# Where two buffers begin: padding ahead of y and of the sums of x in an encoder kernel

## The chip, the cores and the metric

The kernel runs on one core of a Trainium2 chip. The metric is the device time of one execution in microseconds; the median of three runs stands for a kernel. One further execution was taken with the hardware profiler, and the rows below come from it.

## The reference

The reference is the trunk of an encoder with two layers on x of 256 tokens by 1024 channels, all in float32. Each layer adds three terms to x:

```
x = x + 0.5 * swiglu(rmsnorm(x), w_gate, w_up, w_down)     # 1024 -> 2816 -> 1024
x = x + mixer(rmsnorm(x))
x = x + 0.5 * swiglu(rmsnorm(x), w_gate, w_up, w_down)
# swiglu(h) = (silu(h @ w_gate) * (h @ w_up)) @ w_down
```

The mixer of the first layer has one input projection to 2560 columns, a gated part with a 128 by 128 spatial matrix, dilated attention with 8 heads, and an output projection. The mixer of the second layer takes centred averages over windows of 2, 4, 8 and 16 tokens minus the token itself, maps each of four groups of channels by a matrix, and scales. The four networks (swiglu) are most of the work.

## The kernel before, in words

**Numbers.** TensorE runs on float32r operands. To keep float32 accuracy each operand is split into a high part and the rest (ScalarE copies the high part, VectorE subtracts it), and each product is three matmuls: high by high, high by rest, rest by high. `mm3` (line 756) has the weights stationary and 256 tokens moving; `mm3x` (line 763) has 128 tokens stationary and 512 columns of weights moving.

**Weights.** 147 chunks of 1 MB come from memory through SyncE's queue into six buffers `raw`; they are split into four pairs `wh`, `wl` of 8192 bytes per partition. x is kept split in `xh`, `xl`.

**The networks.** `ffn` (line 771 ff.) goes through the 22 blocks of 128 hidden columns by a plan of letters. H takes two blocks in the plain way: x stationary, gate and up columns of the weights moving, 512 at a time. S (`seven`, line 899) takes four blocks with seven products in place of eight, as Strassen and Winograd do: four of the seven products have **sums of x** (`combine`, line 712) as their stationary operand. These sums, four pairs of high part and rest, lie in a buffer named `combos`. There are 15 S blocks; each has 4 products x 4 blocks of rows x 3 matmuls with sums. The results become **y**, the hidden activations, transposed by TensorE (`turned`, line 809) and split into a buffer named `yb`. `down` (line 840) multiplies y by w_down with `mm3`: y moves, the weights are stationary.

**Other users of the two buffers.** In the even mixer (line 1011 ff.) `combos` holds queries, keys, values and gates, and `yb` the input of the output projection, which again moves against stationary weights. In the odd mixer (line 1246 ff.) `yb` holds the tokens' projections and `combos` the pooling matrix.

**Order.** A planner (class `Order`) emits the program. It estimates the time of every instruction from its count of elements, keeps a clock for each engine and puts each engine's instructions in the order in which their inputs are due. It knows nothing of addresses.

**Layout.** Buffers come from pools. Pools lie behind one another in each partition in the order in which they are opened; every buffer is rounded up to 32 bytes. A pool with bufs=n has n copies of each name, used in turn. The pools and their buffers, in bytes per partition:

| pool, in order | buffers |
|---|---|
| cst | raw 6 x 8192, wh and wl 4 x 2 x 8192, xh, xl, xg 8192 each, vec 240, X 8192, ident 512, mixer_consts 8192, acc 2048, ones 4, mhalf 64 |
| tmp, each twice | sq 2048, v 8, rs_y 64, rs_a 64, rs_r 64, half 16, ss 64, ssv 64, one 4 |
| tiny | st 24, four times |
| t2k_pool | t2k 2048, eight times |
| shared | yb 16384, combos 16384 |

`v` takes the mean square in a norm (line 667), `ssv` the same in the mixer, `one` is written once and never read (line 1210).

Of the kernel before, what the change touches and what calls it, by code (L numbers as in the profile page):

```python
# [9 lines left out]
F32 = mybir.dt.float32  # L10
F32R = mybir.dt.float32r
# [4 lines left out]
P = 128  # L16
D = 1024
S = 256
FF = 2816
KD = D // P  # L20
KF = FF // P
NT = S // P
# [16 lines left out]
EXTRA_AT = 2 * 33 + 33 + 14 + 1  # L39
PLANS = ("HHHHSSSH", "HHSSSSH", "HHSSSSH", "HHSSSSH")  # L40
ADD_ISSUE, ADD_TIME, ADD_LAG = 1.4, 5.9, 6.0


V_NORM = 0
# [43 lines left out]
class Order:  # L88
# [13 lines left out]
    def task(self, eng, fn, *deps, can=None, urgent=0.0, idle=0.0):  # L102
        t = Task(eng, fn, deps, can, urgent, idle)
        self.late[eng].append(t)
        return t
# [57 lines left out]
    def need(self, task, what=""):  # L163
        if task is not None:
            self.wait(lambda: task.end is not None and task.end <= self.t, what)
# [217 lines left out]
def tile_encoder(ctx: ExitStack, tc: tile.TileContext, x, w, vecs, qk_gain, w_sp, b_sp, rope, mask, pool_op, eye, out):  # L383
    nc = tc.nc

    cst = ctx.enter_context(tc.tile_pool(name="cst", bufs=1))
    tmp = ctx.enter_context(tc.tile_pool(name="tmp", bufs=2))
    tiny = ctx.enter_context(tc.tile_pool(name="tiny", bufs=4))
    t2k_pool = ctx.enter_context(tc.tile_pool(name="t2k_pool", bufs=8))
# [4 lines left out]
    xh = cst.tile([P, KD, S], F32R, name="xh")  # L394
    xl = cst.tile([P, KD, S], F32R, name="xl")
    xg = cst.tile([P, KD, S], F32, name="xg")
    shared = ctx.enter_context(tc.tile_pool(name="shared", bufs=1))
    ctx.enter_context(tc.manual_schedule())

    O = Order(nc)  # L400
# [8 lines left out]

    def t2k(a, b):  # L410
        return t2k_pool.tile([P, a, b], F32, name="t2k")

    def bank():
        return psum_a.tile([P, 512], F32, name="bank")

    def bank2():
        return psum_b.tile([P, 512], F32, name="bank2")
# [166 lines left out]
    ps = bank2()  # L584
    for _ in range(WARM):
        nc.tensor.matmul(ps[:, :S], lhsT=warm[:, :P], rhs=warm, start=True, stop=True)
    mhalf = cst.tile([P, 16], F32, name="mhalf")
    nc.gpsimd.memset(mhalf, -0.5)

    def mixer_loads():  # L590
# [20 lines left out]
    class Norm:  # L611
# [37 lines left out]
        def square(self, i, *deps, urgent=0.0, idle=0.0):  # L649
            sq = []  # L650

            def square():
                sq.append(self.acc if i == 0 else t2k(2, S))
                A.activation(sq[0], X[:, 2 * i:2 * i + 2], AF.Square)

            t = task("A", square, *deps, urgent=urgent, idle=idle)
            if i:
                t = task("V", lambda: V.tensor_add(self.acc, self.acc, sq[0]), t, urgent=urgent, idle=idle)
            self.summed.append(t)
# [4 lines left out]
                    E.matmul(ps[:, t:t + 1], lhsT=self.acc[:, j, t * P:(t + 1) * P], rhs=ones, start=j == 0, stop=j == 1)  # L664

        def mean(self, ps):
            self.v = tmp.tile([P, NT], F32, name="v")
            V.tensor_scalar(self.v, ps[:, :NT], 1.0 / D, EPS, op0=OP.mult, op1=OP.add)

        def columns(self):  # L670
# [41 lines left out]
        def combine(self, idle):  # L712

            a11, a12 = xg[:, :4, :P], xg[:, 4:, :P]
            a21, a22 = xg[:, :4, P:], xg[:, 4:, P:]
            made, used = [], []
            combos = self.sums_of_x = shared.tile([P, 8, 4, P], F32R, name="combos")

            def add(make, *deps):
                i = len(made)  # L720
                s = []

                def fn():
                    s.append(t2k(4, P))
                    make(s[0])
                    used.append(s)
                    if len(used) == 4:
                        W.raw.lend(XG, xg_raw, O.clock["V"])

                v = task("V", fn, *deps, *self.gained, idle=idle)  # L730
                h = task("A", lambda: A.activation(combos[:, 2 * i], s[0], AF.Copy), v, idle=idle)
                l = task("V", lambda: V.tensor_sub(combos[:, 2 * i + 1], s[0], f32(combos[:, 2 * i])), h, idle=idle)
                made.append(l)
                return s, v

            s1, v1 = add(lambda s: V.tensor_sub(s, a22, a21))
            s2, v2 = add(lambda s: V.scalar_tensor_tensor(s, s1[0], -1.0, a11, op0=OP.mult, op1=OP.subtract), v1)
            add(lambda s: V.tensor_sub(s, a11, a21))
            add(lambda s: V.scalar_tensor_tensor(s, s2[0], -1.0, a12, op0=OP.mult, op1=OP.subtract), v2)
            self.combos = made  # L740
# [22 lines left out]
    def mm3x(ps, xh, xl, wh, wl, first, last, more=False):  # L763

        E.matmul(ps, lhsT=xh, rhs=wh, start=first, stop=False, skip_group_check=more)
        E.matmul(ps, lhsT=xh, rhs=wl, start=False, stop=False, skip_group_check=more)
        E.matmul(ps, lhsT=xl, rhs=wh, start=False, stop=last, skip_group_check=more)
        O.run()


    def ffn(n, f, plan, nxt, store=False, soon=(), after_last_sums=None, squares_first=False):
# [5 lines left out]
            return ring.get()  # L777

        n.columns_soon(ring)
        yb = shared.tile([P, 2, 2, 4, S], F32R, name="yb")  # L780
        tok = [slice(t * P, (t + 1) * P) for t in range(NT)]

        def rows(u, k):
# [205 lines left out]
        for i in range(5):  # L989
            if i < 4:  # L990
                d = 2 * i
# [19 lines left out]
    def even_mixer(n, units, nxt):  # L1011
        B = Blocks(W, units)
        arena = shared.tile([P, 4096], F32, name="combos")
        cat = shared.tile([P, 2, KD, S], F32R, name="yb")
        ch, cl = cat[:, 0], cat[:, 1]
        used = [0]

# [11 lines left out]
        def at(step, *tasks):  # L1029
            B.at(step, *tasks)  # L1030
# [87 lines left out]
        def spatial(g, step):  # L1118
            a = {}

            def mix():
                ps = bank2()
                for t in range(NT):
                    E.matmul(ps[:, t * P:(t + 1) * P], lhsT=gv[t][:, g * P:(g + 1) * P], rhs=wsp[:, g, :],
                                     start=True, stop=True)
                m = t2k(NT, P)
                V.scalar_tensor_tensor(m, ps[:, :S].rearrange("p (t s) -> p t s", t=NT),
                                               vec[:, V_SGU + g:V_SGU + g + 1],
                                               bsp[:, g, None, :].to_broadcast([P, NT, P]), op0=OP.mult, op1=OP.add)
                a[0] = t2k(1, S)[:, 0]  # L1130
                V.tensor_mul(a[0], u[:, g], m.rearrange("p t s -> p (t s)"))
                A.activation(ch[:, g], a[0], AF.Copy)

            at(step, mix)
            at(step + 1, lambda: V.tensor_sub(cl[:, g], a[0], f32(ch[:, g])))
# [71 lines left out]
            at(26 + 2 * g, gate)  # L1207
        for g in range(GROUPS):
            spatial(g, 33 + 2 * g)
        one = tmp.tile([P, 1], F32, name="one")  # L1210
        at(36, lambda: A.activation(one, ones, AF.Exp))
        psv = []
        for t in range(NT):
# [14 lines left out]
        for i in range(KD // 2):  # L1228
# [10 lines left out]
            t = task("V", add, urgent=1.2)  # L1239
# [5 lines left out]

    def odd_mixer(n, units, nxt):
        B = Blocks(W, units)
        hw = shared.tile([P, NT, D], F32, name="yb")
        banks = []
        for g in range(4):  # L1250
            ps = bank()
            if g == 3:
                n.columns()
            need(n.ok[2 * g + 1], "x")
            wh, wl = B.take(4)
            for t in range(NT):
                for k in range(2):
                    kk, s, c = 2 * g + k, slice(t * P, (t + 1) * P), slice(k * 256, (k + 1) * 256)
                    mm3x(ps[:, t * 256:(t + 1) * 256], n.h[:, kk, s], n.l[:, kk, s], wh[:, c], wl[:, c], k == 0, k == 1)
            banks.append(ps)  # L1260
        B.close()
        for g in range(4):
            c = slice(g * 256, (g + 1) * 256)
            A.activation(hw[:, 0, c], banks[g][:, :256], AF.Copy, scale=n.col[:, 0:1])
            V.tensor_scalar(hw[:, 1, c], banks[g][:, 256:], n.col[:, 1:2], None, op0=OP.mult)
        m = Norm(nxt)
        op = extra[0].rearrange("p (t g s) -> p t g s", t=NT, g=4)
        first = P - max(WINDOWS) // 2
        for i in range(KD // 2):
            ps = bank2()  # L1270
            for e in (2 * i, 2 * i + 1):
                c, o = slice(e * P, (e + 1) * P), e % 2 * S
                E.matmul(ps[:, o:o + S], lhsT=hw[:, 0, c], rhs=op[:, 0, e // 2, :], start=o == 0, stop=False)
                E.matmul(ps[:, o + first:o + S], lhsT=hw[:, 1, c], rhs=op[:, 1, e // 2, first:], start=False,
                         stop=o > 0)
                O.run()

            def add(e, ps=ps):
                o = e % 2 * S
                V.scalar_tensor_tensor(X[:, e], ps[:, o:o + S], vec[:, V_POOL + e:V_POOL + e + 1], X[:, e],  # L1280
                                       op0=OP.mult, op1=OP.add)

            ts = [task("V", lambda e=e, add=add: add(e), urgent=0.6) for e in (2 * i, 2 * i + 1)]
            m.pair(i, *ts, urgent=0.6)
            m.square(i, *ts)
        return m
# [121 lines left out]
```

## Time and profile before

| | us |
|---|---|
| median of three runs | 844.29 |
| lowest and highest | 843.77, 845.03 |
| the profiled execution | 845.57 |
| its span, first to last instruction | 843.8 |
| TensorE busy in it | 831.0 |
| VectorE, ScalarE busy | 694.2, 530.5 |

A page of the profile gives busy times by engine, a row of 40 slices, DMA queues, the chain of work that ended last and the costliest groups of instructions. In the rows, PE is TensorE, PEld its loads of stationary operands, DVE is VectorE, ACT ScalarE, POOL GpSimd and SP SyncE. Nearly every instruction has line 196, a helper that records all operations, so rows are told apart by the names of their tiles: `bank<-wh,combos` is a matmul into a bank of the accumulator with wh moving and combos stationary (the moving operand is named first). The end of a matmul is modelled; its start is not.

### The profile page before, as it was taken

Reading aid. Unit: us, or ns where it says so; the run is one execution under the profiler, and the core shown is the slowest. Engines: PE = TensorE matmul, PEld = TensorE weight load, DVE = VectorE, ACT = ScalarE, POOL = GpSimd, SP = SyncE. Lnnn points to the kernel's source line nnn. Section 1 sums busy time; section 2 is a strip of 40 time slices with the busy share of each in tenths; the row PEclk is TensorE's granted clock in tenths of the full one; section 3 lists DMA queues with packets and bytes.
Section 4 is the critical chain, followed back from the end, with each engine's and each line's share of the span. In section 5 each row is a group of like instructions: output and inputs, shape, how many; then the busy total and the mean of one; then the engine's idle time right before and its main releaser. Section 6 shows DMA issues by size and latency. Waiting matters only on the chain.

```text
span 843.8 us, 12378 instructions
## 1 busy us (share of the span) xinstructions
PE 831.0 (98%) x4980; PEld 730.1 (87%) x4980; DVE 694.2 (82%) x655; ACT 530.5 (63%) x544; POOL 67.3 (8%) x53
## 2 busy tenths in 40 slices
PE   7999999999999999999999999999999999999998
PEld 6888888998887988898899888888889788889888
DVE  5956998968877689999986789998967899998972
ACT  7836676556648586756754676766755576765740
POOL 0110000002400011000000100010000100001000
PEclk9999999999999999999999999999999999999999
DMA  9999997965443788999988798999896398999901
GB/s 311 376 334 230 259 288 211 336 250 191 158 150 101 201 243 239 270 305 266 321 285 241 219 239 227 296 293 305 239 371 180 133 248 246 287 318 288 274 3 50
DMA packets 110714, 206.37 MB, mean 245 GB/s; under 512 B 5440, under 2 KB 26816, under 8 KB 108608
## 3 DMA queue, kind: packets, MB, share of 16 engines
q1 hardware_dynamic: 93728, 173.59, 60.1%
q0 software_dynamic: 15840, 31.46, 20.9%
q8 instruction: 39, 0.64, 0.3%
q10 hardware_dynamic: 1088, 0.52, 0.2%
q14 instruction: 19, 0.16, 0.1%
HBM read 204.50 MB, written 1.05 MB: 244 GB/s over the span
## 4 chain that ended last, share of the span: by engine, by line
PE 93%; DVE 3%; ACT 2%; issue 1%; DMA 1%; POOL 0%; SPq 0%; ACTq 0%; POOLq 0%
PE bank L196 93%; DVE wl L196 1%; DVE t2k L196 1%; ACT wh L196 1%; ACT t2k L196 1%; DMA raw<-w_in 1%; DMA X<-x_in 0%; DVE xl L196 0%; ACT L196 0%; DVE yb L196 0%; ACT xh L196 0%; DVE acc L196 0%; POOL rs_y L196 0%; DVE X L196 0%; ACT acc L196 0%
## 5 line engine op out<-in xcount | busy, mean ns | idle before, releaser
L196 DVE TENSOR_TENSOR wl<-raw,wh 128x2048 fp32r<-128x2048 f32 (+2 forms) x159 | 354.7, 2247 | 41.2 <-ACT wh L196 41.1
L196 ACT ACTIVATE wh<-raw 128x2048 fp32r<-128x2048 f32 (+2 forms) x159 | 297.5, 1880 | 108.9 <-PE bank L196 75.0
L196 PE MATMUL bank<-yb,wh 128*128 128x256 f32 x1536 | 275.0, 281 | 0.0
L196 PEld LDWEIGHTS bank<-yb,wh 128*128 128x128 f32 x1536 | 236.7, 188 | 5.0 <-issue 1.0
L196 PE MATMUL bank<-yb,wl 128*128 128x256 f32 x768 | 214.4, 279 | 0.0
L196 PE MATMUL bank<-wh,xh 128*128 128x512 f32 (+1 forms) x484 | 189.4, 391 | 0.9 <-ACT wh L196 0.7
L196 PE MATMUL bank<-wl,xh 128*128 128x512 f32 (+1 forms) x484 | 187.2, 387 | 1.7 <-DVE wl L196 1.7
L196 PE MATMUL bank<-wh,xl 128*128 128x512 f32 (+1 forms) x484 | 187.3, 387 | 0.0
L196 PE MATMUL bank<-wh,combos 128*128 128x512 f32 x480 | 160.9, 398 | 0.0
L196 PEld LDWEIGHTS bank<-yb,wl 128*128 128x128 f32 x768 | 144.3, 188 | 0.0
L196 PEld LDWEIGHTS bank<-wl,xh 128*128 128x128 f32 x484 | 91.0, 188 | 19.7 <-DVE wl L196 2.8
L196 PEld LDWEIGHTS bank<-wh,combos 128*128 128x128 f32 x480 | 90.2, 188 | 19.9
L196 PEld LDWEIGHTS bank<-wh,xl 128*128 128x128 f32 x484 | 90.9, 188 | 18.9
L196 PEld LDWEIGHTS bank<-wh,xh 128*128 128x128 f32 x484 | 91.0, 188 | 18.8 <-ACT wh L196 1.7
L196 PE MATMUL bank<-wl,combos 128*128 128x512 f32 x240 | 95.4, 397 | 0.0
L196 POOL DMA_DIRECT2D raw<-w_in x23 | 29.6, 1288 | 390.5 <-DMA raw<-w_in 134.2
L196 ACT ACTIVATE wh<-mixer_consts 128x2048 fp32r<-128x2048 f32 x22 | 42.1, 1914 | 26.9 <-PE bank L196 19.8
L196 DVE TENSOR_TENSOR wl<-mixer_consts,wh 128x2048 fp32r<-128x2048 f32 x22 | 50.3, 2286 | 10.1 <-ACT wh L196 10.1
L196 PEld LDWEIGHTS bank<-wl,combos 128*128 128x128 f32 x240 | 45.1, 188 | 11.4 <-DVE wl L196 2.1
L196 ACT ACTIVATE t2k<-bank 128x512 f32<-128x512 f32 x53 | 31.4, 593 | 32.0 <-PE bank L196 31.4
L196 ACT ACTIVATE t2k<-bank,rs_r 128x256 f32<-128x256 f32 (+1 forms) x51 | 28.0, 569 | 36.8 <-PE bank L196 36.4
L196 ACT ACTIVATE yb<-bank 128x512 fp32r<-128x512 f32 (+1 forms) x48 | 27.8, 579 | 26.0 <-PE bank L196 26.0
(94 smaller groups left out, 638.7 us busy)
## 6 DMA issues: line engine op xcount, KB each, us to landing
raw<-w_in SPq DMA_DIRECT2D x69, 1024.0 KB, 7.6
raw<-w_in SPq DMA_DIRECT2D x71, 512.0 KB, 8.1
raw<-w_in POOLq DMA_DIRECT2D x23, 1024.0 KB, 13.0
mixer_consts<-w_in SPq DMA_DIRECT2D x13, 1024.0 KB, 7.6
raw<-w_in SPq DMA_DIRECT2D x38, 256.0 KB, 6.2
raw<-w_in SPq DMA_DIRECT2D x23, 384.0 KB, 6.1
xg<-w_in SPq DMA_DIRECT2D x8, 1024.0 KB, 9.8
raw<-w_in SPq DMA_DIRECT2D x8, 768.0 KB, 7.5
```

The costliest lines, as they stand in the source:

```text
L196: return f(*args, **kw)
```

## The change

The pool `shared` is opened straight behind `cst`, ahead of `tmp`. `mhalf`, the last buffer of `cst`, becomes 96 bytes longer, and the buffer of y 64 bytes longer at its end; neither extra part is used. y's buffer gets one size for all its users, and each takes a view of it. To make room, `v` and `one` lose their own buffers and take those of `ssv`.

```diff
+AHEAD_Y, AHEAD_COMBOS = 96, 64
...
     cst = ctx.enter_context(tc.tile_pool(name="cst", bufs=1))
+    shared = ctx.enter_context(tc.tile_pool(name="shared", bufs=1))
     tmp = ctx.enter_context(tc.tile_pool(name="tmp", bufs=2))
...
-    shared = ctx.enter_context(tc.tile_pool(name="shared", bufs=1))
...
+    def y_buffer(dtype):
+        return shared.tile([P, 16 * S + AHEAD_COMBOS // 4], dtype, name="yb")[:, :16 * S]
...
-    mhalf = cst.tile([P, 16], F32, name="mhalf")
+    mhalf = cst.tile([P, 16 + AHEAD_Y // 4], F32, name="mhalf")
...
-            self.v = tmp.tile([P, NT], F32, name="v")
+            self.v = tmp.tile([P, NT], F32, name="ssv")
...
-        yb = shared.tile([P, 2, 2, 4, S], F32R, name="yb")
+        yb = y_buffer(F32R).rearrange("p (b h k s) -> p b h k s", b=2, h=2, k=4)
...
-        cat = shared.tile([P, 2, KD, S], F32R, name="yb")
+        cat = y_buffer(F32R).rearrange("p (h k s) -> p h k s", h=2, k=KD)
...
-        one = tmp.tile([P, 1], F32, name="one")
+        one = tmp.tile([P, NT], F32, name="ssv")[:, :1]
...
-        hw = shared.tile([P, NT, D], F32, name="yb")
+        hw = y_buffer(F32)[:, :NT * D].rearrange("p (t d) -> p t d", t=NT)
```

## Rows read from the trace of the kernel before

**Rows 1.** The page, busy time by engine; clock of TensorE and DMA in 40 slices
```profile
PE 831.0 (98%) x4980; PEld 730.1 (87%) x4980; DVE 694.2 (82%) x655; ACT 530.5 (63%) x544; POOL 67.3 (8%) x53
PEclk9999999999999999999999999999999999999999
DMA  9999997965443788999988798999896398999901
```

**Rows 2.** The page, the chain that ended last, share by engine
```profile
PE 93%; DVE 3%; ACT 2%; issue 1%; DMA 1%; POOL 0%; SPq 0%; ACTq 0%; POOLq 0%
```

**Rows 3.** The waits of TensorE (waiting instruction <- releaser: us, times, longest)
```profile
PE bank L586 <- ACT sq L583: 2.5, 1, 2.5
PE bank L196 <- DVE t2k L196: 2.4, 3, 1.1
PE bank L196 <- DVE wl L196: 1.7, 3, 0.8
PE bank L196 <- ACT yb L196: 1.3, 1, 1.3
PE bank L196 <- ACT wh L196: 0.7, 1, 0.7
```

**Rows 4.** Timeline of TensorE: start us, us, instruction; x stationary, 512 columns
```profile
63.96 0.39 PE L196 MATMUL bank<-wh,xh 128*128 128x512 f32 x1
...
67.59 0.39 PE L196 MATMUL bank<-wl,xh 128*128 128x512 f32 x1
```

**Rows 5.** Timeline of TensorE, x and weights with 256 columns
```profile
648.06 0.28 PE L196 MATMUL bank<-wl,xh 128*128 128x256 f32 x1
...
651.77 0.28 PE L196 MATMUL bank<-wh,xl 128*128 128x256 f32 x1
```

**Rows 6.** Timeline of TensorE, sums of x stationary, 512 columns
```profile
506.40 0.39 PE L196 MATMUL bank<-wh,combos 128*128 128x512 f32 x1
...
512.00 0.28 PE L196 MATMUL bank<-yb,wh 128*128 128x256 f32 x1
```

**Rows 7.** Timeline of TensorE, y moving; a trio is two rows
```profile
832.77 0.40 PE L196 MATMUL bank<-yb,wh 128*128 128x256 f32 x2
833.00 0.28 PE L196 MATMUL bank<-yb,wl 128*128 128x256 f32 x1
...
839.42 0.40 PE L196 MATMUL bank<-yb,wh 128*128 128x256 f32 x2
```

**Rows 8.** Groups of TensorE: tiles, shape, count | busy us, mean ns | idle
```profile
L196 PE MATMUL bank<-yb,wh 128*128 128x256 f32 x1536 | 275.0, 281 | 0.0
L196 PE MATMUL bank<-yb,wl 128*128 128x256 f32 x768 | 214.4, 279 | 0.0
L196 PE MATMUL bank<-wh,combos 128*128 128x512 f32 x480 | 160.9, 398 | 0.0
L196 PE MATMUL bank<-wl,combos 128*128 128x512 f32 x240 | 95.4, 397 | 0.0
L196 PE MATMUL bank<-ident,t2k 128*128 128x128 f32 x224 | 33.9, 274 | 2.4 <-DVE t2k L196 2.4
```

**Rows 9.** Timeline of TensorE, four transposes behind one another; one takes 0.274 (rows 8)
```profile
52.83 0.60 PE L196 MATMUL bank<-ident,t2k 128*128 128x128 f32 x4
```

**Rows 10.** Tiles rs_y, one, mhalf: xcount: ns min/median/max, first and last start us
```profile
L196 POOL TENSOR_TENSOR rs_y<-ssv,mhalf x3: 1635/3276/3345, 210.4 to 234.0; 128x16 f32<-128x16 f32 x2, 128x8 f32<-128x8 f32 x1
L196 ACT ACTIVATE one<-ones x1: 205/205/205, 248.0 to 248.0; 128x1 f32<-128x1 f32 x1
L588 POOL MEMSET mhalf<- x1: 116/116/116, 0.8 to 0.8; 128x16 f32 x1
```

**Rows 11.** The stretch 320 to 460 us: busy us of each engine, clock, DMA share
```profile
core 0: us, PE busy (x) PEld busy (x) DVE busy (x) ACT busy (x) POOL busy (x), PEclk, DMA share, GB/s
320.00:460.00 140.00, 139.59 (x824) 122.49 (x823) 122.37 (x79) 90.31 (x71) 7.67 (x6) 1.00 0.93 276
```

## The prediction

> **What bounds the kernel now.** I read the page first: TensorE is busy 98% of the span, VectorE 82%, and the DMA engines are busy in most slices [rows 1]. The chain that ended last lies on TensorE for 93% [rows 2], and TensorE's own waits come to 8.6 us in all [rows 3]. So the time is set by how fast TensorE works off its queue, and only a change in the distance from one matmul to the next can move the end by much. The durations in the table of groups do not give that distance, because matmuls overlap (a 512-column one is shown with 390 ns and the next begins after 227). I therefore took stretches of the timeline in which one kind of matmul follows itself, and divided the time between the first and the last start by the steps.
>
> [...]
>
> Each matmul streams its moving operand while the next stationary operand is loaded. [...]
>
> **Where the buffers begin.** The pools lie behind one another, buffers rounded up to 32 bytes, so places modulo 256 can be added up from the code. From raw0 to acc all sizes are multiples of 256 (vec's 240 bytes with rounding), so weights, xh and xl begin at one place, which I call 0. Behind them come ones (32) and mhalf (64), then the pool tmp with v 64, rs_y, rs_a and rs_r 128 each, half 64, ss and ssv 128 each, one 64 (832 together), then st 128. That is 1056, or 32 modulo 256: y begins at 32, and so do the sums, since y's buffer is a multiple of 256. The difference moving minus stationary is 0 for x, +32 for y, and -32 (224) for the sums, where the roles are exchanged. [...]
>
> After the change, shared lies straight behind cst: ones 32 and the longer mhalf 160 put y at 192. Its buffer is now 64 bytes longer, so the sums begin at 256, which is 0. **The sums of x thus come to the very place of the weights**, where x is; y goes from +32 to +192, a difference that no row of the trace has.
>
> **The change part by part.**
> *Sums.* 480 + 240 = 720 matmuls have the sums stationary [rows 8]. At difference 0, as x has it, each step is 226.9 in place of 233.3 ns: 720 x 6.4 = 4.6 us less. The two kinds are the same in columns, roles and strides of whole 256 bytes, so I take the x row as it stands. Bounds: nothing (if it is not the place that makes the difference) and 4.6.
> *y.* 1536 + 768 = 2304 matmuls have y moving [rows 8], so 1 ns is 2.3 us. The price at +192 is not in the trace. [...] Where neighbour and slope disagree, I take the row of the same instructions, 116.7, and 0 us, and carry both ends into the range.
> *The smaller edits.* v and one now use the two buffers of ssv. The instructions stay the same; a new wait could only be on a reader two uses back. The last root from ssv starts at 234.0 us and takes 3.3, one is written at 248.0 [rows 10], so 10 us cover it; without that cover, one would cost ScalarE a wait of up to 3.3 us, and what is queued behind it. The memset of mhalf has 40 columns for 16: it took 116 ns at 0.8 us, long before TensorE starts, and is covered by the first loads. [...] No DMA, no engine's order and no wait is touched, since the planner counts elements and does not know addresses.
>
> *What is late next.* If TensorE gets faster, the splits of weights must keep up. In the second network, 320 to 460 us, VectorE is busy 122.4 of 140 us, TensorE 139.6, the DMA engines 0.93 [rows 11]. Its 192 matmuls with sums save 1.2 us there, which lifts VectorE from 87 to 88%: this gain is not given back, but one of ten or more would meet a DMA share near 1.
>
> **Sum.** The profiled execution took 845.57 us, 843.8 of it the span and 1.8 around it; 845.57 - 4.6 + 0 = 841.0. It stands 1.3 above the median of 844.29; on the median's footing the forecast is 839.7.
>
> [...]
>
> **Rivals.**
> [...]
> 2. *Slower: y collides more.* The place is y's moving read in the matmuls of down and of the output projection. At 119.7 ns, the excess that x has, it costs 2304 x 3.0 = 6.9 us, less 4.6: 846.6. [...] It decides from 118.7 ns upward, where 2304 x 2.0 equals the sums' gain. For: 224 is the nearest difference seen. [...]
> 3. *Nothing.* The differences seen come from roles or row counts and not from places (or the layout is not what I added up): 844.3. [...] Against: the sums and x, equal in columns, in roles and in the order of the three matmuls, differ by 6.4 ns a step, and I find nothing but their place that tells them apart.
>
> **How the numbers follow.** Forecast (sums gain, y within 0.8 ns of its row): 0.32, 838 to 842. Rival 1: 0.26. Rival 2: 0.32, of which a third at 855 or more. Rival 3: 0.10. The range reaches to half of rival 1 (829) and takes in the milder part of rival 2 (853): some 0.17 is left out. About 0.2% (1.7 us) is what a measurement of this kernel can tell from no change. Faster by more than that: forecast and rival 1, 0.58; slower 0.30, rival 2 without its smallest cases; the same 0.12.
>
> **What would show it.** In the timeline after: sums at 227 ns a step (if 233, the place is not the cause; if above, the sums did not land at 0); y's trios at 350 ns (340 for rival 1, 359 and more for rival 2); x at 227 and the 256-column x at 120 as before; TensorE's waits still below 10 us. It is wrong if y moves by over 1 ns, and wrong in its reason if the sums keep 233.

## The result and the profile after

| us | before | after |
|---|---|---|
| median of five runs each, side by side | 845.03 | 839.60 |
| lowest and highest | 843.77, 846.61 | 838.79, 841.06 |
| ratio, 95% interval | | 0.9938 [0.992, 0.9957] |
| the profiled execution | 845.57 | 839.6 |
| its span | 843.8 | 837.8 |

The change makes the kernel 0.6% faster, at the predicted time. The page of the changed kernel, busy time by engine and the chain that ended last (compare [rows 1, 2]):

```profile
PE 824.2 (98%) x4980; PEld 727.8 (87%) x4980; DVE 693.6 (83%) x655; ACT 530.6 (63%) x544; POOL 67.3 (8%) x53
...
PE 89%; DMA 4%; DVE 3%; ACT 2%; issue 1%; SPq 0%; POOL 0%; ACTq 0%; POOLq 0%
```

TensorE still sets the time, with the same 4980 matmuls in 824.2 in place of 831.0 us: 6.8 less. Its waits, as engine, tile and line, releaser, us in all, times, longest:

```profile
PE bank L200 <- DVE t2k L200: 2.5, 2, 1.4
PE bank L593 <- ACT sq L590: 2.5, 1, 2.5
PE bank L200 <- DVE wl L200: 1.7, 3, 0.8
PE bank L200 <- ACT yb L200: 1.3, 1, 1.3
PE bank L200 <- ACT wh L200: 1.2, 1, 1.2
PE bank L200 <- ACT t2k L200: 0.2, 1, 0.2
```

They come to 9.4 us where [rows 3] have 8.6. So 6.8 - 0.8 = 6.0 us, which is the whole difference of the spans: the time came out of the matmuls, and next to nothing was given back. The stretch of 320 to 460 us (columns as in [rows 11]) shows why:

```profile
320.00:460.00 140.00, 139.96 (x846) 124.47 (x845) 123.69 (x81) 90.37 (x73) 7.67 (x6) 1.00 0.95 280
```

TensorE does 846 matmuls in it where it did 824; VectorE, at 123.7 of 140 us, and the DMA engines, at 0.95, follow without a wait showing.

Which matmuls became shorter shows in the groups (those of [rows 8]):

```profile
L200 PE MATMUL bank<-yb,wh 128*128 128x256 f32 x1536 | 273.2, 281 | 0.0
L200 PE MATMUL bank<-yb,wl 128*128 128x256 f32 x768 | 214.2, 279 | 0.0
...
L200 PE MATMUL bank<-wh,combos 128*128 128x512 f32 x480 | 158.4, 393 | 0.0
L200 PE MATMUL bank<-wl,combos 128*128 128x512 f32 x240 | 94.1, 392 | 0.2
```

The sums lose 2.5 + 1.3 us and y 1.8 + 0.2, although y was taken as unchanged. The steps tell more. Timeline of TensorE after, the first and last rows of stretches (start, us, instruction):

```profile
51.16 0.40 PE L200 MATMUL bank<-yb,wh 128*128 128x256 f32 x2
...
52.93 0.60 PE L200 MATMUL bank<-ident,t2k 128*128 128x128 f32 x4
53.28 0.48 PE L200 MATMUL bank<-yb,wh 128*128 128x256 f32 x2
...
53.72 0.39 PE L200 MATMUL bank<-yb,wh 128*128 128x256 f32 x2
...
57.12 0.39 PE L200 MATMUL bank<-wh,xh 128*128 128x512 f32 x1
...
63.94 0.39 PE L200 MATMUL bank<-wh,xh 128*128 128x512 f32 x1
...
67.56 0.39 PE L200 MATMUL bank<-wl,xh 128*128 128x512 f32 x1
...
502.78 0.39 PE L200 MATMUL bank<-wh,combos 128*128 128x512 f32 x1
...
508.22 0.40 PE L200 MATMUL bank<-yb,wh 128*128 128x256 f32 x2
...
511.05 0.39 PE L200 MATMUL bank<-wh,combos 128*128 128x512 f32 x1
...
646.05 0.28 PE L200 MATMUL bank<-wl,xh 128*128 128x256 f32 x1
...
647.61 0.28 PE L200 MATMUL bank<-wh,xl 128*128 128x256 f32 x1
...
826.67 0.39 PE L200 MATMUL bank<-yb,wh 128*128 128x256 f32 x2
...
833.47 0.39 PE L200 MATMUL bank<-yb,wh 128*128 128x256 f32 x2
```

Divide each stretch by its steps:

- x stationary, 63.94 to 67.56, 16 steps: 226.3 ns, the 226.9 that [rows 4] have in 16, within the rounding of the starts; x with 256 columns, 646.05 to 647.61, 13 steps: 120.0, where [rows 5] have 119.7 in 31. Nothing was done to these.
- Sums, 502.78 to 508.22, 24 steps: 226.7 ns, where the same products had 233.3 in 24 [rows 6].
- y behind those sums, 508.22 to 511.05, 24 steps: 117.9 ns. y behind x, 51.16 to 52.93, 15 steps: 118.0. But y behind four transposes, 53.72 to 57.12, 30 steps: 113.3, and in `down` of the last network, 826.67 to 833.47, 60 steps: 113.3, where [rows 7] have 116.7 in 57. **The same matmuls, with the same buffers, now run in one of two trains, 113 or 118 ns**, and what precedes a train goes with the choice.

### The profile page after: what moved, and what is told of

Read it like the earlier page. It is cut to its first block, busy times and chain, and to the rows that moved or that the text cites. A ratio compares the mean times of both kernels' runs of the same rounds, so it can differ in the third digit from the quotient of the medians.

```text
span 837.8 us, 12377 instructions
## 1 busy us (share of the span) xinstructions
PE 824.2 (98%) x4980; PEld 727.8 (87%) x4980; DVE 693.6 (83%) x655; ACT 530.6 (63%) x544; POOL 67.3 (8%) x53
## 4 chain that ended last, share of the span: by engine, by line
PE 89%; DMA 4%; DVE 3%; ACT 2%; issue 1%; SPq 0%; POOL 0%; ACTq 0%; POOLq 0%
PE bank L200 89%; DMA xg<-w_in 3%; DVE wl L200 2%; DVE t2k L200 1%; ACT wh L200 1%; ACT t2k L200 1%; DMA X<-x_in 0%; DMA raw<-w_in 0%; DVE raw L200 0%; DVE xl L200 0%; ACT L200 0%; SPq L200 0%; DVE yb L200 0%; ACT xh L200 0%; DVE acc L200 0%
## 5 line engine op out<-in xcount | busy, mean ns | idle before, releaser
L200 PE MATMUL bank<-wh,combos 128*128 128x512 f32 x480 | 158.4, 393 | 0.0
L200 DVE TENSOR_TENSOR wl<-mixer_consts,wh 128x2048 fp32r<-128x2048 f32 x22 | 50.3, 2286 | 10.5 <-ACT wh L200 10.5
```

Source lines behind the costliest of these rows:

```text
L200: return f(*args, **kw)
```

## The experiments

For each run I also took the difference of every two matmul starts that follow each other in the trace, and put it down to the first of the two. "Mean" is over steps under 150 ns for y and under 260 ns for the sums; "total" is over all steps. Places are bytes modulo 256 from the weights' place. Before has means of 116.8 (y) and 233.1 (sums), totals of 275.0 and 170.2 us; after 116.0 and 227.8, 273.3 and 166.8. A total also holds some 37 longer steps of y, first steps behind transposes and waits; they come to 8.6 to 12.0 us, differently in each run, so a difference of 1 or 2 us in y's total alone says little. By its mean, y gained 0.8 ns in 2266 short steps, 1.8 us.

The theory to be tested: each of the two buffers has a price of its own, set by its place. The rivals: that the gain comes from the moved pool and the smaller buffers; that only one of the two moves matters; and, on the form of the price, that one curve of the difference moving minus stationary serves whichever operand is in the buffer.

**Both places put back,** the pool's move and the smaller buffers kept: paddings such that y and the sums begin at 32, as before.

```diff
-AHEAD_Y, AHEAD_COMBOS = 96, 64
+AHEAD_Y, AHEAD_COMBOS = 192, 0
```

> Everything of the change is kept (the pool of y and sums ahead, the shared small buffers), only the paddings are 192 and 0 bytes, so that y and the sums begin 32 bytes past the weights' place modulo 256, as before. Theory (the step from one matmul to the next depends on the difference of the two operands' places modulo 256): sums 233.3 ns a step, y 116.7, time as before, 845.0 within 1.7. Rival (the gain is from the new order of the pools or the shared small buffers): sums 227, time 839.6.

Measured: 844.24 us, ratio 0.9994 [0.9984, 1.0004]; y 116.8, sums 233.2 ns, as before. (y's total is 273.3 us here too, as after the change: it is the longer steps that are shorter, by 1.7 us.) The gain is the two places, and the smaller edits cost and give nothing that can be told.

**One place at a time.** y alone at 192, the sums at 32:

```diff
-AHEAD_Y, AHEAD_COMBOS = 96, 64
+AHEAD_Y, AHEAD_COMBOS = 96, 96
```

> y at 192 as after the change, the sums at 32 as before it. Theory: sums 233.3 ns a step, y about 116 as after; time 839.6 + 720 x 6.4 ns = 844.2. Rival (most of the gain is y's): 840 or 841.

The sums alone at 0, y at 32 (the sums in a pool of their own ahead of `shared`, and 32 unused bytes between them and y):

```diff
-AHEAD_Y, AHEAD_COMBOS = 96, 64
+AHEAD_Y, AHEAD_COMBOS = 160, 0
...
+    sums = ctx.enter_context(tc.tile_pool(name="sums", bufs=1))
     shared = ctx.enter_context(tc.tile_pool(name="shared", bufs=1))
+    shared.tile([P, 8], F32, name="ahead")
...
-            combos = self.sums_of_x = shared.tile([P, 8, 4, P], F32R, name="combos")
+            combos = self.sums_of_x = sums.tile([P, 8, 4, P], F32R, name="combos")
...
```

The two other users of `combos` take the new pool too.

> The sums at 0 as after the change, y at 32 as before it. Theory: sums 227 ns a step, y 116.7; time 845.0 - 4.6 = 840.4. Rival (most of the gain is y's): 843 to 845.

Measured: y alone 839.75 us, 0.9935 [0.9921, 0.9949]; the sums alone 842.16, 0.9966 [0.9956, 0.9977]; the median of before beside both was 844.93. So y alone gives 5.2 us, the sums alone 2.8, together 8.0; the change, which has both, gives 5.4. The intervals keep this apart: 0.9935 x 0.9966 = 0.9901, below the interval of the change. **The two gains don't add up.** Timeline of TensorE with y alone moved, a train of 24 sums and the 24 steps of y behind it:

```profile
82.49 0.39 PE L200 MATMUL bank<-wh,combos 128*128 128x512 f32 x1
...
88.08 0.40 PE L200 MATMUL bank<-yb,wh 128*128 128x256 f32 x2
...
90.81 0.39 PE L200 MATMUL bank<-wh,combos 128*128 128x512 f32 x1
```

The sums take 5.59 us (232.9 ns a step), y behind them 2.73 (113.8). With the sums alone moved:

```profile
82.06 0.39 PE L200 MATMUL bank<-wh,combos 128*128 128x512 f32 x1
...
87.50 0.40 PE L200 MATMUL bank<-yb,wh 128*128 128x256 f32 x2
...
90.30 0.39 PE L200 MATMUL bank<-wh,combos 128*128 128x512 f32 x1
```

The sums take 5.44 us (226.7), y 2.80 (116.7). And with both moved, in the changed kernel, the trains shown above took 5.44 and 2.83. Behind sums at 0, y at 192 falls into its slow train (26 of 30 such trains; the other four have transposes among the dozen matmuls ahead of them); behind sums at 32 it falls into its fast one (30 of 30). In totals: y takes 269.7 us with y alone, 273.3 with both, so 3.6 us of y's gain go where the sums gain 3.4. The longer steps are 10.4 and 10.5 us in these two, so here the totals compare.

**Both 256 bytes earlier,** to see whether the places repeat: `vec` goes from `cst` to a later pool, and all behind it moves down by its 256 bytes.

```diff
-    vec = cst.tile([P, V_N], F32, name="vec")
+    vec = tiny.tile([P, V_N], F32, name="vec", bufs=1)
```

> vec (256 bytes) lies behind y and the sums in place of ahead of them, so that both begin 256 bytes earlier against the weights: the same modulo 256, another place modulo 512. Theory with 256 bytes: sums 227 ns a step, y about 116, time as after, 839.6. Rival (the pattern repeats at 512 bytes or more): sums or y change by 3 ns or more a step; for the sums at 233 the time would be 844.

Measured: 838.61 us in one run; y 116.1, sums 227.8 ns, as after. This shift by a whole 256 bytes changed nothing in the steps.

**Other places for both.** Four pairs of paddings; the diffs are the one line with the two numbers, and the comments give the places.

```diff
+AHEAD_Y, AHEAD_COMBOS = 160, 0    # y 0, sums 0
...
+AHEAD_Y, AHEAD_COMBOS = 32, 32    # y 128, sums 160
...
+AHEAD_Y, AHEAD_COMBOS = 64, 32    # y 160, sums 192
...
+AHEAD_Y, AHEAD_COMBOS = 128, 0    # y 224, sums 224
```

> Paddings 160 and 0: y and the sums both at the weights' place (0). Theory (the step follows the difference moving minus stationary modulo 256, whoever moves): y 120 ns a step, as x with 256 columns, sums 227; y costs 2304 x 4 = 9 us more than after, time about 848. Rival (which operand moves and how many columns decides too): y at 113 to 117.

> Paddings 32 and 32: y at 128, sums at 160 (differences +128 and +96, both unseen). [...]

> Paddings 64 and 32: y at 160, sums at 192 (differences +160 and +64). [...] Theory with one curve for both: the sums at +64 lie below their value at +32.

> Paddings 128 and 0: y at 224, sums at 224 (differences -32 and +32), the mirror of before. Theory with one curve whoever moves: y has the 20 ns that the sums had at -32, 126.7 ns a step, 24 us more than after; the sums have the 10 ns that y had at +32, 223.3. Rival (each role has a curve of its own): y well under 126.7.

Measured, one run each, 845.47 for before beside them:

| y, sums at | us | y, ns a step | sums, ns a step | totals of y and sums, against before | time, against before |
|---|---|---|---|---|---|
| 0, 0 | 849.12 | 119.7 | 228.2 | +6.5 - 3.1 = +3.4 | +3.7 |
| 128, 160 | 850.69 | 119.1 | 233.2 | +4.3 + 0.1 = +4.4 | +5.2 |
| 160, 192 | 846.25 | 118.6 | 229.5 | +3.2 - 2.2 = +1.0 | +0.8 |
| 224, 224 | 849.59 | 118.3 | 233.0 | +3.9 - 0.2 = +3.7 | +4.1 |

The two totals account for each time to within 0.8 us, so the steps of y and of the sums are what the places change. Three of the four are slower than before. A single time says little, as before itself took 843.5 to 850.2 us in its runs, but the means repeat: y at 32 has 116.8 ns in all three profiled runs that have it, sums at 32 have 233.0 to 233.2 and at 0 227.8 to 228.2.

y at the weights' place, timeline of the run with both at 0 (sums, then y):

```profile
82.87 0.39 PE L200 MATMUL bank<-wh,combos 128*128 128x512 f32 x1
...
88.31 0.40 PE L200 MATMUL bank<-yb,wh 128*128 128x256 f32 x2
...
91.18 0.40 PE L200 MATMUL bank<-wh,combos 128*128 128x512 f32 x1
```

y takes 2.87 us for 24 steps, 119.6 ns: the step of x with 256 columns, 119.7 [rows 5], as the difference of 0 says. Both at 224:

```profile
83.21 0.39 PE L200 MATMUL bank<-wh,combos 128*128 128x512 f32 x1
...
88.80 0.40 PE L200 MATMUL bank<-yb,wh 128*128 128x256 f32 x2
...
91.64 0.39 PE L200 MATMUL bank<-wh,combos 128*128 128x512 f32 x1
```

The expectation's 126.7 and 223.3 start from 20 and 10 ns, the author's estimates, which no run shows. The rows give nearly the same: by one curve for both roles, y at 224 would stand above x as the old sums did (233.3 for 226.9, so 6.4), at 119.7 + 6.4 = 126.1 ns, and the sums at 224 (a difference of 32) below x as the old y did (116.7 for 119.7, so 3.0), at 226.9 - 3.0 = 223.9. They have 2.84 / 24 = 118.3 and 5.59 / 24 = 232.9. **That idea falls:** a place has one price for the moving operand and another for the stationary one.

**What stands ahead of y.** y stays at 192; the sums go to 192 and to 96 (there in a pool ahead of y's, as when they moved alone), and a third run has y at 96 for its curve (sums at 128). The comments give the places.

```diff
+AHEAD_Y, AHEAD_COMBOS = 96, 0    # y 192, sums 192
...
+AHEAD_Y, AHEAD_COMBOS = 0, 0     # y 192, sums 96: sums in the pool ahead, as above
+    shared.tile([P, 24], F32, name="ahead")
...
+AHEAD_Y, AHEAD_COMBOS = 0, 32    # y 96, sums 128
```

> Paddings 96 and 0: y at 192 as after the change, the sums at 192 too (229 ns a step there, by the run with y at 160). Theory now: y at 192 has two steady trains, 113 and 118 ns a step, and the instruction ahead of a train decides which; after sums at 0 it is 118, after sums at 32 it was 113. If the sums at 192 lead to 113 as those at 32 did: y 114.4 on average, time 839.75 - 720 x 4 ns = 836.9. Rival (only sums at 32 do so): y 116, time 839.6 + 720 x 2 ns = 841.

> y at 192, the sums at 96, a place not yet seen, their buffer ahead of y's. Theory: sums between 227 and 233 ns a step, y between 114.4 and 116 on average, as the train that they lead to; time between 836 and 844. It settles whether any place serves the sums better than the weights' own. Rival (the two buffers do not act on one another): y 116.0 whatever the sums do.

> Paddings 0 and 32: y at 96, the sums at 128, the last places that memory has room for but y at 64. No number beyond the span seen so far: y 113 to 120 ns a step, sums 227 to 233; time 838 to 851.

Measured: 839.61 us, 0.9940 [0.9924, 0.9956], with y 114.9 and sums 229.4 ns; 844.01, 0.999 [0.9979, 1.0], with 115.9 and 233.4; and 851.15 in one run, with 119.9 and 232.6. Behind sums at 192 about 18 of 30 trains of y are fast; behind sums at 96, which step at 233 as those at 32 do, 26 of 30 are slow. So it isn't the pace of the sums that decides which train y falls into, and not y's place alone; the place of what ran before goes into it, or something that moved with that place, such as the order of the two buffers. With y at 192 the sums at 0, at 32 and at 192 all end at 839.6 to 839.8 us: what a place saves in the sums it takes from y. The run with y at 96 is the slowest of all.

**Sums split between two places.** If y falls into its fast train behind sums at 32, and the sums are fastest at 0, then only those sums that stand ahead of y need 32: first and fourth pair at 0, second and third at 32, y at 192.

```diff
-            combos = self.sums_of_x = shared.tile([P, 8, 4, P], F32R, name="combos")
+            room = shared.tile([P, 8 * 512 + 8], F32R, name="combos")
+            places = (0, 512, 2056, 2568, 3080, 3592, 1024, 1536)
+            combos = self.sums_of_x = [room[:, a:a + 512].rearrange("p (k s) -> p k s", k=4) for a in places]
...
```

The lines left out take the sums from this list.

> The kernel after the change, but the second and third of the four sums begin 32 bytes past the weights' place, the first and fourth at it. The second and third are the ones whose products stand ahead of y's matmuls. Theory (the train that y falls into is decided by what stands ahead of it): the y trains behind sums all run at 113 to 114 ns a step, as in the run with y alone, where after the change 26 of 30 ran at 118; that is 26 trains x 35 x 4.4 ns = 4.0 us less; half of the sums' matmuls at 233 for 227 ns cost 360 x 6 = 2.2 us; time 839.6 - 1.8 = 837.8. Rival (the place of all four sums, or of t2k, decides): y unchanged at 116.0 on average, time 839.6 + 2.2 = 841.8.

Measured: 838.36 us, 0.9913 [0.9895, 0.9931] beside 844.97. Timeline, 24 sums of two products, then y:

```profile
82.49 0.39 PE L200 MATMUL bank<-wh,combos 128*128 128x512 f32 x1
...
84.98 0.63 PE L200 MATMUL bank<-wh,combos 128*128 128x512 f32 x2
...
88.01 0.40 PE L200 MATMUL bank<-yb,wh 128*128 128x256 f32 x2
...
90.75 0.39 PE L200 MATMUL bank<-wh,combos 128*128 128x512 f32 x1
```

The first 11 steps, at 0, take 2.49 us (226.4 ns), the other 13 take 3.03 (233.1), and y follows in 2.74 (114.2). All 30 trains of y behind sums are fast. The totals are y 270.5 and sums 168.6 us: 4.5 and 1.6 less than before, 6.1 in all. y's short steps alone lose 6.1 us; its longer ones gain 1.6, and TensorE's waits for `t2k` were 4.0 us in this run where [rows 3] have 2.4. It is the best median of the study, but its interval overlaps that of the change, so that it beats before is shown and that it beats the change is not.

## Why the prediction was right, and where it was not

The time came out as forecast (839.7 for 839.60); the parts of the sum did not, so a match this close is luck. The gain was forecast as 4.6 us and measured 5.4 side by side, where before itself ran 0.7 us slower than in the three runs, 844.29, on which the forecast stands.

- *What bounds.* Right: TensorE's busy time fell by 6.8 us and the span by 6.0.
- *Where the buffers begin.* Right: put back, they give the time of before (0.9994), and 256 bytes earlier they give the steps of after.
- *The term of the sums.* The place was the cause: 233.3 became 226.7 ns in settled trains. The size was 4.6 us and measured 170.2 - 166.8 = 3.4 by all steps, 2.8 by the run with the sums alone (844.93 to 842.16). The mean over all trains is 227.8 and not 226.9, since some trains begin with steps of 228 to 236 ns before they settle; one settled row was multiplied by all 720.
- *The term of y.* Forecast 0; it was -1.8 us in the change (0.8 ns in 2266 steps) and -5.2 when moved alone. This is the step that failed: y at 192 is better than at 32, which was rival 1's case, with its trios of 340 ns in the trains at 113.3. The change shows only a third of that, because more than half of the trains run at 118. By the forecast's own sign of being wrong, y moving by over 1 ns, the settled trains are wrong (113.3 and 117.8 for 116.7); the mean over all, 116.0 for 116.8, stays within it. No row of before shows two trains for one place, and the sum took the two terms as independent: alone they give 8.0, together 5.4. The gain of y that was left out and the oversized gain of the sums made up for one another, which is luck. The neighbour and the slope between which the forecast took 0 were the author's estimates, and no run shows such a slope: y's own prices at 224, 0 and 32 are 118.3, 119.7 and 116.8 ns, no even fall that goes on to 192.
- *The bounds of y.* The two ends that go into the range, and the 855 of rival 2, were the author's estimates, which no run shows for y. The worst y of seven places is 119.9 ns and the best train has 113.3; the times of the changed kernel and of the twelve runs, 838.4 to 851.2 us, lie inside the range of 829 to 853. Outside the trains a step can be far shorter: in the trace of before, the step from the last of four transposes to the next matmul is 28 or 29 ns in 51 of 54 cases, with one of 200 ns or more behind it.
- *The smaller edits, and t2k.* Right: the smaller edits are 0 within the interval of 0.9984 to 1.0004; the transposes of t2k, which moved as well, have a median step of 109 ns before and after.
- *What is late next.* Right: waits of 9.4 us, under the 10 forecast.
- *Rival 2* was the fate of other places: y at 0 has the 119.7 ns that it was priced at, and that run is 3.7 us slower than before, where the rival had 2.3 slower (846.6 against 844.29). It lost at 192, where y is under 118.7.
- *Rival 3* fell with the run that puts both back: 844.24 us, where the same edits with the other two places have 839.60. If no place mattered, no run here should have differed; the changed kernel and the twelve runs, which have the same matmuls, lie as far apart as 838.4 and 851.2 us.

**What stays open** is why. The runs give prices by place and role, a repeat at 256 bytes (y 116.1 and sums 227.8 ns in that run, 116.0 and 227.8 after), and a dependence on what ran before; no run shows what in the memory or in TensorE makes the steps. The weights begin at one place in every run, so it is open too whether a price belongs to the distance between the two operands or to the place of each. The totals explain the times to one or two microseconds: against the profiled execution of before (845.57), on which they rest, the profiled one with the sums alone moved took 2.1 us less for 1.6 less in the totals, the one with y at 96 5.6 more for 5.1 more, but the one with the sums at 96 0.4 more for 1.2 less. y at 64 was not tried.

## What to carry to other kernels

Where TensorE is busy 98% of the time, take the distance from start to start of each kind of matmul from the timeline; if kinds of one shape differ, look at where their operands begin modulo 256 bytes: one buffer at 192 in place of 32 was worth 5 us of 845 here, and the worst pair of places cost 6. Try the places of the moving and of the stationary operand separately and then together: here the gains did not add up, and the pace of one buffer's matmuls depended on what ran ahead of them. A term taken from one settled stretch came out too large for the sums, 4.6 us where all steps show 3.4; the first steps of a train, and what they do to the next one, have to be counted from all steps.

## What was not expected of the hardware

- **One place, two trains.** With y at 192, trios of y take 340 ns or 353 ns, for whole trains of 24 steps and more, made of the same instructions. In the change, those right behind transposes were mostly fast (21 of 24), those behind x slow (10 of 11), those behind sums went by the sums' place; with y alone moved, 17 of 24 behind transposes were fast. y at 128 has two as well, trios of 360 ns and of 355 to 357.
- **A grid of 6.67 ns.** Many settled trains repeat on multiples of it: x with 512 columns 226.7 ns = 34 x 6.67, with 256 columns 120.0 = 18, a pair of sums at 32 466.7 = 70, a trio of y at 192 340 = 51 or 353.3 = 53. Not all do: a trio of y at 32 takes 350 ns, 52.5 of them. In the trace of before, the starts of 54 settled trains of x also lie on one phase of that grid, to within 1.1 ns, over the whole 844 us. No run tells where the grid comes from.
- **Of the seven places tried for each, the weights' own is the best for a stationary operand and among the worst for a moving one.** Means over all trains, some from one run. Sums: 0 (227.8 to 228.2), 192 (229.4 to 229.5), 128 (232.6), then 32, 96, 160 and 224 at 233. y: 192 (114.2 to 116.1), 32 (116.8), 224 (118.3), 160 (118.6), 128 (119.1), 0 (119.7), 96 (119.9).
